# A hybrid attention block on one Trainium2 core: low-rank codes in 2 passes of 16, statistics ahead of the last depth step, ten leading matmuls of constants, a filled slot and one more pool

## The chip, the core and the metric

The kernel runs on one core of one Trainium2 chip. The core has TensorE (PE) for matrix products, VectorE (DVE) and ScalarE (ACT) for element work, GpSimd (POOL), which does next to nothing here, and SyncE (SP), on whose queue nearly all DMA transfers are issued. SBUF is the on-chip memory of 128 partitions that the engines work on, PSUM holds what PE writes, in banks of 128 x 512 float32. The metric is the time of one execution on the device in microseconds (us), the median of several runs. All runs shown are of one launch that computes one layer for 1024 tokens.

## What is computed

One encoder layer in float32 on x of 1024 tokens by 1024 features. The reference, cut to what matters here:

```python
h = _rms_norm(x, norm_mix_g[l])
proj = h @ w_in[l]
(g_q, g_k, g_v, g_r, g_lr_f, g_lr_b, s_q, s_k, s_v, gate_a, gate_b) = jnp.split(proj, split_at, axis=-1)
y_gla = _gla_branch(g_q, g_k, g_v, g_r, g_lr_f, g_lr_b, ...) @ w_o_gla[l]
y_swa = _swa_branch(s_q, s_k, s_v, ...) @ w_o_swa[l]
merged = jax.nn.sigmoid(gate_a) * y_gla + jax.nn.sigmoid(gate_b) * y_swa
x = x + merged @ w_out[l]
h2 = _rms_norm(x, norm_ffn_g[l])
gu = h2 @ w_ffn_in[l]
x = x + (jax.nn.silu(gu[..., :D_FF]) * gu[..., D_FF:]) @ w_ffn_out[l]
```

Inside the GLA branch the gate of each direction is `z = lr @ up + bias`, with `lr` the low-rank code of a token: 16 numbers for the forward and 16 for the backward direction, so 32 columns of `w_in`. Its log-sigmoid is summed along chunks of tokens and scales q and k of four heads. The SWA branch is windowed attention with 8 query heads.

## The kernel before

Matrix products are kept at float32 precision by splitting each operand into a high part of type float32r and a low part, the rest. A product is three matmuls (`mm3`, lines 74 to 77): high by high, low by high, high by low. All take 128 rows of depth, mostly 128 x 512 results; the kernel has 7880. Weights arrive as units of 128 x 512 through `wunit` (lines 62 to 69): SP loads `wr` (4 buffers), ACT copies the high part `wh` (5), DVE subtracts to get the low part `wl` (5). x lies transposed, as `xh[k][s]` and `xl[k][s]`: depth step k of 8 by token half s of 2.

The stages, in order:

- The **lead**. ACT and DVE split x depth step by depth step, with the gain of the norm, while PE multiplies it with the weights of q and k of head 0 into four banks `bq[m][s]` (m is 0 for q, 1 for k). x itself is squared on ACT (`x_square`) and summed on DVE into `acc`. The norm's factor is applied to results, so it is needed only then: `norm_stats` (lines 117 to 121) multiplies `acc` with a matrix of ones, one fp32 matmul for each half, and `rsqrt` makes `rstd`. Eight small matmuls (`vt`) give the same factor by token, `rstdt`. The low-rank codes (`lr_mm`, lines 247 to 253) stand around this: the 32 columns are repeated three times to 96, in two weight units of four depth steps; each step and half takes three matmuls, 48 in all, 24 ahead of the statistics and 24 behind. `lr_out` multiplies with `rstd` and writes `lrS`: rows 0 to 31 the high part, 32 to 63 the low part, 64 to 95 the high part again, and two rows of ones for the bias. The gates' matmul then reads all 98 rows of `lrS` against `upS`, which holds the up-projection as high, high and low. The first gates' matmul of the program is a mark in what follows.
- The **GLA slots**. The other projections are generators in the list `dense`, 2400 matmuls, which `fill(n)` draws from one by one. The GLA of 4 heads by 8 chunks is cut into small steps, and `slot(stages, n)` (line 230) runs the steps of one time slot with n dense matmuls spread between them: 40 in slots 0 to 5, 31 in slots 6 to 34, and 18 in slots 35 to 44. Ahead of slot 0 stand 24 dense matmuls. A slot without a step returns without any fill. There are two such: slot 1, and slot 43, between the last step back through the chunks (`g_back_out`, whose last ACT instruction scales `ob`, line 484) and the last turn (`g_turn`, line 490, whose transposes read `ob`).
- The **SWA slots**, with 60, 46 or 28 dense matmuls each, and what is left of `dense` behind them.
- The **projections of the branches and the output**. `prep_a` (lines 766 to 777) loads the GLA's output `o` and the gate `r` for each of eight depth steps into pairs of buffers (`lo`, `lr`), which lie in memory that the SWA stage frees, and writes the parts `oah` and `oal` that the next matmuls read.
- **FFN in**, by seven products of half blocks in place of eight (Strassen's way): x1 is combined into the operands 11, 21, T1, 22, T2, T3 and T4, each as high and low parts of four depth steps, 16 KB in a partition. They lie in three pools: `big1` (11, 21; 32 KB), `big2` (T1, 22, T2; 48 KB) and `big3` (T3, T4). For each of 22 feature tiles `ffn_in` runs T1, T2, 21, 11 of the next tile, T3, 22, T4.
- **FFN out**, likewise, in groups of 132 matmuls (line 1029). Once the big pools close, `fo1`, `fo2` and `fo3` take their memory from the same start. `fo1` holds six buffers `hr` for loads of activations (12 KB) and eleven weight tiles `a11` (22 KB), 34 KB; `fo2` and `fo3` hold the parts `hh` and `hl` (lines 1001 and 1002) and further weights.

The order of PE is the order of the code (`manual_schedule`). The orders of ACT, DVE and SP are made by the tile scheduler. Each engine works its own queue strictly in order and waits at semaphores for the others. A tile in memory that another pool had before waits for that pool's last reader there.

Of the kernel before, what the change touches and what calls it, by code (L numbers as in the profile page):

```python
# [8 lines left out]
F32 = mybir.dt.float32  # L9
# [5 lines left out]
P = 128  # L15
# [8 lines left out]
NB = 7  # L24
PAD = 672
# [4 lines left out]
def body(tc, i, out):  # L30
    nc = tc.nc
    with ExitStack() as root:
# [90 lines left out]
        def fgroup(units, xa, xb, nk):  # L123

            b = [mmtile(), mmtile()]
            k = 0
            for src, ku in units:
                h, l = wunit(src, ku * P)
                for kk in range(ku):
                    c = slice(kk * P, (kk + 1) * P)  # L130
                    st, sp = k == 0, k == nk - 1
                    mm(b[0], h[:, c], xa[k][0], st, False)
                    mm(b[0], h[:, c], xb[k][0], False, False)
                    mm(b[1], h[:, c], xa[k][1], st, False)
                    mm(b[1], h[:, c], xb[k][1], False, False)
                    mm(b[0], l[:, c], xa[k][0], False, sp)
                    mm(b[1], l[:, c], xa[k][1], False, sp)
                    k += 1
            return b

# [89 lines left out]
        def slot(stages, n):  # L230

            stages = [f for f in stages if f]
            done = 0
            for j, f in enumerate(stages):
                f()
                t = n * (j + 1) // len(stages)
                fill(t - done)
                done = t
# [8 lines left out]
        def lr_mm(b, u):  # L247
            h, l = wunit(i["w_lr"][u], 384)
            for kk in range(4):
                k = u * 4 + kk  # L250
                c = slice(kk * 96, (kk + 1) * 96)
                for s in range(2):
                    mm3(b[s][:96], h[:, c], l[:, c], xh[k][s], xl[k][s], k == 0, k == KT - 1)

        def lr_out(b):
            lrf = ip.tile([96, T], F32, tag="lrf", name="lrf")
            for s in range(2):
                c = slice(s * HT, (s + 1) * HT)
# [21 lines left out]

        with tc.manual_schedule(engines={mybir.EngineType.PE}):
            bq = [[mmtile(), mmtile()] for _ in range(2)]

# [3 lines left out]
            for k in range(KT):  # L287
# [924 lines left out]
```

## Time and profile before

| | us |
|---|---|
| median of 3 runs | 1688.89 (1688.65 to 1688.97) |
| span of the profiled execution | 1687.4 |
| PE busy, 7880 matmuls | 1670.9 |
| DVE busy, 2454 instructions | 1181.0 |
| ACT busy, 1939 instructions | 869.3 |

The profile shows one execution. It gives no time of its own for that execution beside the span; the runs lie 1.2 to 1.6 us above it. A matmul's end is modelled in the trace, so PE's busy time says less than the distance between the starts of its matmuls. In the rows of the timeline the first number is the start in us, the second the length, then engine, line, operation, what is written and read with the shape, and in brackets how long the engine was idle before and what released it. Names are those of the program without buffer numbers.

### The profile page before, as it was taken

How to read it: one execution, taken by the hardware profiler on the slowest of the kernel's cores; microseconds unless marked ns; L12 is line 12 of the kernel's file. 1: busy time of each engine (PE TensorE's matmuls, PEld its weight loads, DVE VectorE, ACT ScalarE, POOL GpSimd, SP SyncE). 2: the span in 40 equal slices, each digit the busy share in tenths (PEclk: the TensorE clock that was granted, in tenths of full speed). 3: DMA queues.
4: the chain of work that ended last, by engine and by line, in shares of the span. 5: the costliest groups of instructions: out<-in, count | busy, mean ns of one | idle time of the engine just before them, and what ended most of it. 6: DMA issues, size and time to landing. Idle time of an engine off the chain costs nothing.

```text
span 1687.4 us, 23673 instructions
## 1 busy us (share of the span) xinstructions
PE 1670.9 (99%) x7880; PEld 1390.1 (82%) x7880; DVE 1181.0 (70%) x2454; ACT 869.3 (52%) x1939; POOL 0.2 (0%) x4
## 2 busy tenths in 40 slices
PE   8999999999999999999999999999999999999999
PEld 6788888888788888888888888888888888788887
DVE  7767777764578666546674468987778877779755
ACT  7554767776557656544553466533333333354443
POOL 0000000000000000000000000000000000000000
PEclk9999999999999999999999999999999999999999
DMA  6533434444533233247764645344224443496433
GB/s 197 157 113 109 123 126 140 131 141 125 175 121 118 83 100 96 74 150 245 235 213 146 188 129 187 113 134 134 94 88 156 163 143 132 152 333 200 146 100 119
DMA packets 153738, 245.85 MB, mean 146 GB/s; under 512 B 17582, under 2 KB 43054, under 8 KB 153616
## 3 DMA queue, kind: packets, MB, share of 16 engines
q1 hardware_dynamic: 153616, 244.34, 45.6%
q8 instruction: 62, 1.02, 0.3%
q14 instruction: 60, 0.49, 0.1%
HBM read 177.17 MB, written 67.11 MB: 145 GB/s over the span
## 4 chain that ended last, share of the span: by engine, by line
PE 97%; DVE 2%; ACT 1%; DMA 0%; issue 0%; SPq 0%; ACTq 0%; DVEq 0%
PE mm L72 48%; PE ch L72 9%; PE mm L1029 7%; PE mm L884 6%; PE mm L882 6%; PE mm L883 6%; PE ch L1029 5%; PE ch L884 2%; PE ch L882 2%; PE ch L883 2%; PE ch L664 1%; PE ch L490 0%; PE ch L614 0%; PE ch L405 0%; DVE cs L364 0%
## 5 line engine op out<-in xcount | busy, mean ns | idle before, releaser
L66 ACT ACTIVATE wh<-wr 128x512 fp32r<-128x512 f32 (+1 forms) x256 | 160.1, 628 | 173.6 <-PE mm L72 149.5
L68 DVE TENSOR_TENSOR wl<-wr,wh 128x512 fp32r<-128x512 f32 (+1 forms) x256 | 174.9, 687 | 89.0 <-ACT wh L66 82.2
L72 PE MATMUL mm<-xh,wh 128*128 128x512 f32 x512 | 203.3, 397 | 5.9 <-ACT wh L66 5.9
L72 PE MATMUL mm<-xl,wh 128*128 128x512 f32 x512 | 203.4, 397 | 0.0
L72 PE MATMUL mm<-xh,wl 128*128 128x512 f32 x512 | 169.4, 397 | 0.0
L72 PE MATMUL mm<-wh,xh 128*128 128x512 f32 x320 | 126.7, 396 | 1.9 <-DVE st L146 1.2
L72 PE MATMUL mm<-wl,xh 128*128 128x512 f32 x320 | 127.3, 398 | 0.0
L72 PE MATMUL mm<-wh,xl 128*128 128x512 f32 x320 | 126.4, 395 | 0.0
L72 PEld LDWEIGHTS mm<-xh,wh 128*128 128x128 f32 x512 | 96.7, 189 | 22.4 <-ACT wh L66 5.9
L856 ACT ACTIVATE wh<-ws 128x512 fp32r<-128x512 f32 x88 | 55.7, 634 | 115.2 <-PE mm L883 69.3
L72 PEld LDWEIGHTS mm<-xl,wh 128*128 128x128 f32 x512 | 96.7, 189 | 16.9
L72 PEld LDWEIGHTS mm<-xh,wl 128*128 128x128 f32 x512 | 94.9, 189 | 16.7 <-DVE wl L68 0.2
L856 ACT ACTIVATE wh<-a 128x512 fp32r<-128x512 f32 x66 | 41.9, 635 | 90.9 <-PE ch L1029 42.2
L856 ACT ACTIVATE wh<-wr 128x512 fp32r<-128x512 f32 x52 | 33.0, 635 | 91.1 <-issue 49.5
L857 DVE TENSOR_TENSOR wl<-a,wh 128x512 fp32r<-128x512 f32 x66 | 45.5, 690 | 41.8 <-ACT wh L856 41.6
L72 PEld LDWEIGHTS mm<-wh,xh 128*128 128x128 f32 x320 | 60.2, 188 | 14.0 <-DVE st L146 1.6
L1029 PE MATMUL mm<-hh,wh 128*128 128x512 f32 x176 | 69.3, 394 | 1.6 <-ACT hh L1001 1.6
L1029 PE MATMUL mm<-hl,wh 128*128 128x512 f32 x176 | 69.1, 393 | 0.5 <-DVE hl L1002 0.5
L1029 PE MATMUL mm<-hh,wl 128*128 128x512 f32 x176 | 69.2, 393 | 0.1
L647 ACT ACTIVATE p<-p,nm,rs 128x384 f32<-128x384 f32 (+1 forms) x64 | 42.9, 673 | 50.3 <-DVE nm L641 50.3
L72 PEld LDWEIGHTS mm<-wh,xl 128*128 128x128 f32 x320 | 60.2, 188 | 10.4
L857 DVE TENSOR_TENSOR wl<-ws,wh 128x512 fp32r<-128x512 f32 x88 | 60.3, 685 | 11.9 <-ACT wh L856 11.9
(508 smaller groups left out, 4419.8 us busy)
## 6 DMA issues: line engine op xcount, KB each, us to landing
wr<-in_w_fi_dram SPq DMA_DIRECT2D x102, 256.0 KB, 2.9
wr<-in_w_t_dram SPq DMA_DIRECT2D x80, 256.0 KB, 2.8
wr<-in_w_f_dram SPq DMA_DIRECT2D x64, 256.0 KB, 2.7
B<-c SPq DMA_DIRECT2D x44, 256.0 KB, 2.1
T<-tx SPq DMA_DIRECT2D x44, 256.0 KB, 2.4
a<-in_w_fo_dram SPq DMA_DIRECT2D x44, 256.0 KB, 5.3
hr<-T SPq DMA_DIRECT2D x44, 256.0 KB, 2.7
hr<-B SPq DMA_DIRECT2D x33, 256.0 KB, 4.3
```

The lines of the kernel that those rows point to most:

```text
L66: nc.scalar.activation(h, raw, AF.Copy)
L68: nc.vector.tensor_tensor(l, raw, h.bitcast(F32), op=ALU.subtract)
L72: nc.tensor.matmul(o, a, b, start=start, stop=stop)
L647: nc.scalar.activation(p[:, h, :w], p[:, h, :w], AF.Exp, bias=nm_[:, h:h + 1], scale=a.rs[:, h:h + 1], accum_out=dn[:, h:h + 1])
L664: nc.tensor.transpose(pt[:, h], a.p[:, h, (kb - a.b0) * P:(kb - a.b0 + 1) * P], ident)
L856: nc.scalar.activation(h, src, AF.Copy)
L857: nc.vector.tensor_tensor(l, src, h.bitcast(F32), op=ALU.subtract)
L882: nc.tensor.matmul(o, h[:, c], x[kk][0], start=start and kk == 0, stop=False, skip_group_check=True)
L883: nc.tensor.matmul(o, h[:, c], x[kk][1], start=False, stop=False, skip_group_check=True)
L884: nc.tensor.matmul(o, l[:, c], x[kk][0], start=False, stop=kk == nk - 1, skip_group_check=True)
L1029: nc.tensor.matmul(ys[m], a[:, c], b, start=f0, stop=f1, skip_group_check=True)
```

## The change

There are five parts.

1. The 32 columns of the low-rank codes are loaded once as 128 x 8 x 32 and split into `lrhl`, high and low side by side. For each depth step and half one matmul takes 64 columns (high and low against `xh`) and one 32 columns (high against `xl`): 32 matmuls. `lr_out` then adds rows 32 to 63 to rows 0 to 31, by way of a copy on ACT, before it multiplies with `rstd`, and writes the two high copies and the low part of `lrS`.
2. `norm_stats` stands ahead of depth step 7 of q and k (a new function `qk_mm`), and all of the codes' matmuls come behind that step, in one piece, then `vt`.
3. Ten fp32 matmuls of 128 x 128, ones by ones, stand first on PE. They write a bank that q and k overwrite later.
4. A slot without a step draws its n dense matmuls.
5. T1 lies in a pool of its own, `big4`, between `big1` and `big2`.

The unused function `fgroup` is deleted.

```diff
--- before.py
+++ after.py
@@ -22,6 +22,7 @@
 NFF = 22
 NA = 4
 NB = 7
+WARM = 10
 PAD = 672
 
 QKM = ("q0", "k0", "q1", "k1", "q2", "k2", "q3", "k3")
@@ -119,24 +120,6 @@
                 v = chtile((P, HT))
                 mm(v, ones, acc[:, s * HT:(s + 1) * HT], True, True)
                 rsqrt(rstd[:, s * HT:(s + 1) * HT], v, 1.0 / T, EPS, epst, pool, (P, HT), "rs")
-
-        def fgroup(units, xa, xb, nk):
...
 
         def proj_f_out(name, b):
             for s in range(2):
@@ -231,6 +214,8 @@
 
             stages = [f for f in stages if f]
             done = 0
+            if not stages:
+                fill(n)
             for j, f in enumerate(stages):
                 f()
                 t = n * (j + 1) // len(stages)
@@ -244,21 +229,29 @@
         mask = gc.tile([P, 4, P], F32, tag="mask", name="mask")
         nc.vector.memset(mask, 1.0)
         nc.vector.memset(mask[:, :, 0:1], 0.0)
-        def lr_mm(b, u):
-            h, l = wunit(i["w_lr"][u], 384)
-            for kk in range(4):
-                k = u * 4 + kk
-                c = slice(kk * 96, (kk + 1) * 96)
+        def lr_mm(b):
+            raw = ip.tile([P, KT, 32], F32, tag="lrw", name="lrw")
+            nc.sync.dma_start(out=raw, in_=i["w_lr"])
+            hl = ip.tile([P, KT, 2, 32], FR, tag="lrhl", name="lrhl")
+            nc.scalar.activation(hl[:, :, 0], raw, AF.Copy)
+            nc.vector.tensor_tensor(hl[:, :, 1], raw, hl[:, :, 0].bitcast(F32), op=ALU.subtract)
+            for k in range(KT):
                 for s in range(2):
-                    mm3(b[s][:96], h[:, c], l[:, c], xh[k][s], xl[k][s], k == 0, k == KT - 1)
+                    st, sp = k == 0, k == KT - 1
+                    mm(b[s][0:64], hl[:, k].rearrange("p a b -> p (a b)"), xh[k][s], st, sp)
+                    nc.tensor.matmul(b[s][0:32], hl[:, k, 0], xl[k][s], start=False, stop=sp, skip_group_check=True)
 
         def lr_out(b):
-            lrf = ip.tile([96, T], F32, tag="lrf", name="lrf")
+            lrf = ip.tile([32, T], F32, tag="lrf", name="lrf")
+            lrt = ip.tile([32, T], F32, tag="lrt", name="lrt")
             for s in range(2):
                 c = slice(s * HT, (s + 1) * HT)
-                nc.vector.tensor_tensor(lrf[:, c], b[s][:96], rstd[:96, c], op=ALU.mult)
-            nc.scalar.activation(lrS[0:96], lrf, AF.Copy)
-            nc.vector.tensor_tensor(lrS[32:64], lrf[32:64], lrS[32:64].bitcast(F32), op=ALU.subtract)
+                nc.scalar.copy(lrt[:, c], b[s][32:64])
+                nc.vector.tensor_tensor(lrf[:, c], b[s][0:32], lrt[:, c], op=ALU.add)
+            nc.vector.tensor_tensor(lrf, lrf, rstd[0:32], op=ALU.mult)
+            nc.scalar.activation(lrS[0:32], lrf, AF.Copy)
+            nc.scalar.activation(lrS[64:96], lrf, AF.Copy)
+            nc.vector.tensor_tensor(lrS[32:64], lrf, lrS[0:32].bitcast(F32), op=ALU.subtract)
 
         xr = {}
 
@@ -278,8 +271,15 @@
             if k:
                 nc.vector.tensor_tensor(a, a, sq, op=ALU.add)
 
+        def qk_mm(k, s):
+            c = slice((k % 4) * P, (k % 4 + 1) * P)
+            for m in range(2):
+                mm3(bq[m][s], us[m][0][:, c], us[m][1][:, c], xh[k][s], xl[k][s], k == 0, k == KT - 1)
+
         with tc.manual_schedule(engines={mybir.EngineType.PE}):
             bq = [[mmtile(), mmtile()] for _ in range(2)]
+            for _ in range(WARM):
+                mm(bq[1][1][:, :P], ones, ones, True, True)
 
             x_load(0, 0)
             us = [wunit(i["w_f"][m, 0]) for m in range(2)]
@@ -290,11 +290,10 @@
                         x_load(k + 1, s)
                 if k == 4:
                     us = [wunit(i["w_f"][m, 1]) for m in range(2)]
-                c = slice((k % 4) * P, (k % 4 + 1) * P)
                 for s in range(2):
                     x_tile(k, s)
-                    for m in range(2):
-                        mm3(bq[m][s], us[m][0][:, c], us[m][1][:, c], xh[k][s], xl[k][s], k == 0, k == KT - 1)
+                    if k < KT - 1:
+                        qk_mm(k, s)
             for k in range(KT):
                 for s in range(2):
                     x_square(k, s)
@@ -302,13 +301,14 @@
             tri = load_const(gc, "tri", i["c_tri"], (P, P), U32)
             g2 = load_const(cst, "g2", i["g2"], (P, KT))
             og = load_const(cst, "og", i["og"], (P, 2))
+            norm_stats(acc, ip)
+            for s in range(2):
+                qk_mm(KT - 1, s)
             bl = [chtile((P, 512)), chtile((P, 512))]
-            lr_mm(bl, 0)
-            norm_stats(acc, ip)
+            lr_mm(bl)
             vt = chtile((P, KT, 2))
             for t in range(KT):
                 mm(vt[:, t], acc[:, t * P:(t + 1) * P], ones[:, 0:2], True, True)
-            lr_mm(bl, 1)
             proj_f_out("q0", bq[0])
             proj_f_out("k0", bq[1])
             rsqrt(rstdt, vt[:, :, 0], 1.0 / T, EPS, epst, ip, (P, KT), "rt")
@@ -725,7 +725,7 @@
                 YX["21"].append(bsplit(big1, f"b21{k}", b21))
             elif step == 1:
                 nc.vector.tensor_tensor(b12, b12, b11, op=ALU.subtract)
-                YX["T1"].append(bsplit(big2, f"bt1{k}", b12))
+                YX["T1"].append(bsplit(big4, f"bt1{k}", b12))
                 YX["22"].append(bsplit(big2, f"b22{k}", b22))
                 nc.vector.tensor_tensor(b22, b22, b12, op=ALU.subtract)
                 YX["T2"].append(bsplit(big2, f"bt2{k}", b22))
@@ -846,6 +846,7 @@
         bs.close()
         bigs = ExitStack()
         big1 = bigs.enter_context(tc.tile_pool(name="big1", bufs=1))
+        big4 = bigs.enter_context(tc.tile_pool(name="big4", bufs=1))
         big2 = bigs.enter_context(tc.tile_pool(name="big2", bufs=1))
 
 
@@ -1154,8 +1155,7 @@
     d["w_f"] = _units(np.concatenate(cols, axis=1), 4)
     wt = [w[:, 1024:1536], w[:, 1536:2048], w[:, 4128:4640], w[:, 3104:3616], w[:, 3616:4128]]
     d["w_t"] = np.ascontiguousarray(np.stack([a.reshape(KT, P, 512) for a in wt]))
-    lr = np.tile(w[:, 3072:3104], (1, 3)).reshape(2, 4, P, 96)
-    d["w_lr"] = np.ascontiguousarray(lr.transpose(0, 2, 1, 3)).reshape(2, P, 384)
+    d["w_lr"] = np.ascontiguousarray(w[:, 3072:3104].reshape(KT, P, 32).transpose(1, 0, 2))
     up = np.zeros((98, 2, 512), f)
     for g in range(3):
         up[g * 32:g * 32 + 16, 0] = n["gla_gate_up_fwd"][0]
```

How this moves instructions is seen at three places, with rows of the built programs' orders: line, operation, written<-read, shape. First PE in the lead, before: the end of the first 24 matmuls of the codes, the statistics, and the first of the second 24 (ch_377 and ch_376 are the codes' two banks, ch_408 and ch_418 those of the statistics).

```order
L72 MATMUL ch_377<-xh_97,wh_380 96x512
L72 MATMUL ch_377<-xl_113,wh_380 96x512
L72 MATMUL ch_377<-xh_97,wl_382 96x512
L72 MATMUL ch_408<-acc,ones 128x512
L72 MATMUL ch_418<-acc,ones 128x512
L72 MATMUL ch_428<-ones,acc 128x2 x8
L72 MATMUL ch_376<-xh_98,wh_439 96x512
```

And PE at the statistics now, in depth steps 6 and 7 of q and k (mm_136 to mm_139 are their banks; xh_103 and xl_119 are step 6, xh_104 and xl_120 step 7, of half 1 and half 0).

```order
L73 MATMUL mm_139<-xh_103,wh_258 128x512
L73 MATMUL mm_139<-xl_119,wh_258 128x512
L73 MATMUL mm_139<-xh_103,wl_260 128x512
L73 MATMUL ch_374<-acc,ones 128x512
L73 MATMUL ch_384<-acc,ones 128x512
L73 MATMUL mm_136<-xh_104,wh_252 128x512
L73 MATMUL mm_136<-xl_120,wh_252 128x512
```

Ahead of the statistics stand the q and k matmuls of step 6 now, no longer step 7 and 24 of the codes, and step 7 begins right behind them.

DVE at the last squares, before: the sums into acc, then the codes' low parts, then upS.

```order
L279 TENSOR_TENSOR acc<-acc,sq_353 128x512
L279 TENSOR_TENSOR acc<-acc,sq_356 128x512
L279 TENSOR_TENSOR acc<-acc,sq_359 128x512
L279 TENSOR_TENSOR acc<-acc,sq_362 128x512
L279 TENSOR_TENSOR acc<-acc,sq_365 128x512
L68 TENSOR_TENSOR wl_382<-wr_378,wh_380 128x384
L68 TENSOR_TENSOR wl_441<-wr_437,wh_439 128x384
L318 TENSOR_TENSOR upS<-upr,upS 34x1024
```

The same place of DVE now (sq_351 is the square of step 5, half 1; sq_360 and sq_363 those of step 7, half 0 and half 1; lrw and lrhl hold the columns of the codes).

```order
L272 TENSOR_TENSOR acc<-acc,sq_351 128x512
L237 TENSOR_TENSOR lrhl<-lrw,lrhl 128x8x32
L318 TENSOR_TENSOR upS<-upr,upS 34x1024
L272 TENSOR_TENSOR acc<-acc,sq_354 128x512
L272 TENSOR_TENSOR acc<-acc,sq_357 128x512
L272 TENSOR_TENSOR acc<-acc,sq_360 128x512
L69 TENSOR_TENSOR wl_525<-wr_521,wh_523 128x512
L272 TENSOR_TENSOR acc<-acc,sq_363 128x512
```

The subtractions for the codes and for upS stand ahead of the last four sums, and a weight's subtraction ahead of the very last.

DVE at the border of FFN in and FFN out, before: lines 958 to 969 make the last feature tile's outputs c from u and the products, line 1002 makes the low part of the activations of FFN out, line 857 that of its weights.

```order
L958 TENSOR_TENSOR c_3562_15609<-mm_15529,p_3551_15548 128x512
L961 TENSOR_TENSOR u_3555_15569<-ch_15528,u_3555_15569 128x512
L962 TENSOR_TENSOR u_3555_15569<-u_3555_15569,rstd 128x512
L964 TENSOR_TENSOR u_3555_15569<-u_3555_15569,rstd 128x512
L967 TENSOR_TENSOR c_3568_15649<-mm_15529,p_3529_15440 128x512
L969 TENSOR_TENSOR c_3562_15609<-c_3562_15609,u_3555_15569 128x512
L968 TENSOR_TENSOR c_3568_15649<-c_3568_15649,g_3558_15587 128x512
L1002 TENSOR_TENSOR hl_15687<-hr_15684,hh_15686 128x512
L857 TENSOR_TENSOR wl_15691<-a_3580_15682,wh_15690 128x512
```

DVE at the border now:

```order
L959 TENSOR_TENSOR c_3556_15604<-mm_15524,p_3545_15543 128x512
L858 TENSOR_TENSOR wl_15687<-a_3574_15678,wh_15686 128x512
L858 TENSOR_TENSOR wl_15711<-a_3580_15702,wh_15710 128x512
L962 TENSOR_TENSOR u_3549_15564<-ch_15523,u_3549_15564 128x512
L1003 TENSOR_TENSOR hl_15683<-hr_15680,hh_15682 128x512
L963 TENSOR_TENSOR u_3549_15564<-u_3549_15564,rstd 128x512
L1003 TENSOR_TENSOR hl_15707<-hr_15704,hh_15706 128x512
L1003 TENSOR_TENSOR hl_15734<-hr_15731,hh_15733 128x512
L965 TENSOR_TENSOR u_3549_15564<-u_3549_15564,rstd 128x512
L968 TENSOR_TENSOR c_3562_15644<-mm_15524,p_3523_15435 128x512
L970 TENSOR_TENSOR c_3556_15604<-c_3556_15604,u_3549_15564 128x512
L969 TENSOR_TENSOR c_3562_15644<-c_3562_15644,g_3552_15582 128x512
```

The weights' subtractions (line 858 now) come ahead of line 962, and the activations' (line 1003) right behind it, ahead of the last products of FFN in (968 to 970).

More of the change, by code (lines that the diff above doesn't have):

```diff
@@ L121, in norm_stats @@
                 rsqrt(rstd[:, s * HT:(s + 1) * HT], v, 1.0 / T, EPS, epst, pool, (P, HT), "rs")
-        def fgroup(units, xa, xb, nk):
[L125 to L139, printed above, removed]
         def proj_f_out(name, b):
```

## The prediction

> **What bounds the kernel now.** I read the chain of the page first, then PE's waits, then the clock by stretches, and last the rows around each place that the change touches.
>
> ```profile
> span 1687.4 us, 23673 instructions
> ...
> PE 97%; DVE 2%; ACT 1%; DMA 0%; issue 0%; SPq 0%; ACTq 0%; DVEq 0%
> ```
>
> The chain that ended last is PE for 97% of its length. DVE and ACT matter only where PE waits for them, and these are all of PE's waits (engine, line waited for, us in total, times, longest):
>
> ```profile
> PE mm L72 <- ACT wh L66: 5.9, 1, 5.9
> PE ch L490 <- ACT ob L484: 1.6, 1, 1.6
> PE mm L1029 <- ACT hh L1001: 1.6, 1, 1.6
> PE mm L72 <- DVE st L146: 1.2, 1, 1.2
> PE mm L72 <- DVE st L149: 0.7, 1, 0.7
> PE ch L72 <- DVE rt L96: 0.6, 1, 0.6
> PE mm L1029 <- DVE hl L1002: 0.5, 1, 0.5
> PE ch L72 <- DVE sl L420: 0.3, 1, 0.3
> ```
>
> They come to 12.4 us, of which 5.9 are the start. Beside waits PE loses time where its clock is halved. The windows view gives span and length of a stretch, then busy time with count of PE, PEld, DVE, ACT, POOL, the granted clock, DMA share and GB/s:
>
> ```profile
> 5.87:9.20 3.33, 3.33 (x8) 2.64 (x9) 2.65 (x4) 3.01 (x6) 0.00 (x0) 1.00 1.02 375
> 36.60:40.00 3.40, 2.75 (x21) 2.35 (x20) 1.67 (x4) 1.17 (x4) 0.00 (x0) 0.99 0.29 77
> 40.00:43.40 3.40, 3.40 (x9) 2.22 (x8) 3.30 (x8) 1.32 (x2) 0.00 (x0) 0.50 0.18 67
> 1469.50:1473.60 4.10, 1.92 (x6) 1.14 (x7) 3.47 (x7) 2.74 (x5) 0.00 (x0) 1.00 0.98 353
> 1473.60:1477.00 3.40, 3.40 (x10) 2.62 (x9) 3.40 (x7) 1.57 (x4) 0.00 (x0) 0.50 0.94 280
> ...
> 1504.07 29.92 PE ch L1029 x132
> ```
>
> The last row, from the chain in order of time, is the price of a matmul at full speed: 29.92/132 = 0.2267 us. From 5.87 to 9.20 only 8 ran, 0.42 each: PE starts at half speed. Two later windows of 3.4 us are at clock 0.50, and each follows a stretch in which PE stood or ran tiny matmuls. One such window costs half its length, 1.7 us. So what can be won is some 6.5 us of waits behind the start and 3.4 us of clock, beside matmuls that go away.
>
> **The lead.** The mark is the first matmul of the gates, which reads lrS and upS.
>
> ```profile
> 0.83 0.17 DVE L83 MEMSET ones<- 128x128 f32 x1 [0.83 <-PEq L1200]
> ...
> 26.65 0.39 PE L72 MATMUL mm<-xh,wh 128*128 128x512 f32 x1
> 29.37 0.39 PE L72 MATMUL ch<-xh,wh 128*96 128x512 f32 x1
> 34.91 1.88 PE L72 MATMUL ch<-acc,ones 128*128 128x512 f32 x4
> 37.43 1.95 PE L72 MATMUL ch<-ones,acc 128*128 128x2 f32 x16 [0.65 <-DVE rt L96]
> 53.39 0.40 PE L72 MATMUL ch<-lrS,upS 98*128 98x256 f32 x2
> ```
>
> Step 7 of q0 and k0 takes 29.37 - 26.65 = 2.72 us. The 24 low-rank matmuls of the first half take 34.91 - 29.37 = 5.54, 0.231 each with 96 columns, against 0.2267 with 128: width hardly counts. The 32 passes of 64 and 32 columns I price at 0.231, 7.4 us; if width counted in proportion they would cost 2.8, so the gain of leaving out 16 is 3.7, up to 8.3. I take 3.7, as 96 and 128 columns stand so close.
>
> Now the statistics come before step 7, and need all squares summed. On DVE and ACT (first and only row of each):
>
> ```profile
> 21.47 6.12 DVE L279 TENSOR_TENSOR acc<-acc,sq 128x512 f32<-128x512 f32 x10
> 28.55 1.22 DVE L318 TENSOR_TENSOR upS<-upr,upS 34x1024 fp32r<-34x1024 f32 x1
> 26.68 1.04 ACT L317 ACTIVATE upS<-upr 98x1024 fp32r<-98x1024 f32 x1
> 57.41 0.42 DVE L370 TENSOR_TENSOR e<-cs 128x256 f32<-128x256 f32 x1
> ```
>
> Ten additions run from 21.47, 0.61 each, and ended at 27.6 where nobody waited. In the new order of DVE the subtractions for the codes and for upS stand among them. Six additions end at 25.1; the codes' subtraction of 256 columns costs 0.42 by the last row; upS 1.22 makes 26.7; three more additions 28.6, the last of half 0. The last square of half 1 is late on ACT behind the upS copies (1.04 and another like it), so with a weight subtraction between, its sum is there at 29.8.
>
> PE ends step 6 at 26.65, or up to 1.5 us sooner if the ten leading matmuls take the start's half speed away. I take 1.0 sooner, 25.65, since x is split only about as fast as PE eats it. So **a new wait of some 3 us** stands before the statistics: half 0 28.6 to 29.5 (1.88 for both halves), half 1 to 30.7. What the leading matmuls win is swallowed by this wait: at the mark they are worth nothing. Are they hidden themselves? The nearest row is that of two 128x128 matmuls in 0.44 (at 439.80, below), so ten cost 2.2 us, 4.4 at half speed, from 1.0 (ones written) to 5.4, before 5.87. If each cost as much as one of 512 columns at half speed (1.88), they would end at 19.8, and push PE by 13.9 less the 3 of the wait; I take the nearer row.
>
> Then step 7 ends at 33.4, the codes at 40.8, the token statistics (1.9) at 42.7, the 24 dense matmuls ahead of the mark (5.4) at 48.1. The codes' way to lrS (two copies and additions, a product, two copies, a subtraction, 5.5 to 9 us with what DVE does between) has 7.3: I put the wait at 0.3, from 0 to 2. Mark at 48.4, without loss of clock. The waits for rt and st are gone from the sum: the statistics are done at 30.7, ten microseconds ahead of vt, and q0 and k0 leave their banks meanwhile.
>
> The clock stays. The window 36.60 to 40.00 had 2.75 of PE busy, in 16 tiny pieces besides, and the next was at 0.50. A wait of 3 us leaves PE busier by no more than that, so I expect a halved window behind it, 1.7 us: **mark at 50.1, gain 3.3.** [...]
>
> **The empty slots.** Slot 1 only takes its 40 dense matmuls earlier. Slot 43 stands at the end of the GLA:
>
> ```profile
> 437.76 0.40 PE L72 MATMUL mm<-xh,wh 128*128 128x512 f32 x1
> 439.80 0.44 PE L490 MATMUL ch<-ident,ob 128*128 128x128 f32 x2 [1.64 <-ACT ob L484]
> ```
>
> Between the last dense matmul and the turn PE lost 2.04 - 0.23 = 1.8 us. Now 18 dense matmuls, 4.1 us, stand there: **gain 1.8**, all of it, since the copy of ob needs no more than the 2.04. These 58 matmuls are missing later, in the end in the fill behind the last attention matmul, which falls from 190 to 144 by the new order of PE. That fill covers the preparation of the next stage:
>
> ```profile
> 743.92 0.39 PE L72 MATMUL ch<-ph,vSl 128*128 128x512 f32 x1
> 758.79 0.64 ACT L762 ACTIVATE oah<-lo 128x512 fp32r<-128x512 f32 x1 [0.23 <-DVE lo L776]
> 778.77 0.64 ACT L762 ACTIVATE oah<-lo 128x512 fp32r<-128x512 f32 x1 [1.31 <-DVE lo L776]
> 780.45 0.68 DVE L763 TENSOR_TENSOR oal<-lo,oah 128x512 fp32r<-128x512 f32 x1
> 787.49 0.39 PE L72 MATMUL mm<-oah,wh 128*128 128x512 f32 x1
> ```
>
> The rows are the last attention matmul, the high part of the second and the last of eight depth steps, the last low part, and the first matmul that reads them. The preparation starts when the attention's buffers come free, and ends 37.2 us after 743.92. PE came back after 43.57 (190 of 0.229) and needs the eighth step 21 matmuls, 4.8 us, later still. Now it comes back after 33.0, and needs the eighth at 37.8. That leaves 0.6 us, so I cost it at nothing; without that cover each microsecond that the preparation is longer would count in full.
>
> **The new pool.** At the border of the two FFN stages:
>
> ```profile
> 1460.94 0.39 PE L884 MATMUL mm<-b213h,wl 128*128 128x512 f32 x1
> 1466.38 0.39 PE L884 MATMUL ch<-b223h,wl 128*128 128x512 f32 x1
> 1466.80 0.33 SPq L1010 DMA_DIRECT2D a<-in_w_fo_dram  x1
> 1469.10 0.39 PE L884 MATMUL mm<-bt43h,wl 128*128 128x512 f32 x1
> 1469.83 0.63 ACT L856 ACTIVATE wh<-a 128x512 fp32r<-128x512 f32 x1 [0.93 <-DMA a<-in_w_fo_dram]
> 1471.08 0.50 PE L1029 MATMUL mm<-hh,wh 128*128 128x512 f32 x1 [1.59 <-ACT hh L1001]
> ```
>
> The load of the weight a goes out at 1466.80, as the last reader of 22 ends, because fo1 (34 KB) reached past big1 (32 KB) into the next pool. It lands 3.0 us later; ACT splits a, then hh, and PE starts 1.75 us late, waits again for hl, and gets a halved window. With T1 behind big1, the load waits for 21 (done at 1461.3) and T1, read earlier: 5.4 us sooner, a split by 1465. hh still lies over 22, so it is made from 1466.8 on, by 1467.8; hl, now ahead of the last products on DVE, by 1469.1. PE wants hh at 1469.33 and hl at 1469.56. Both are there: margin 0.5 us. From 1469.33 to 1504.07 are 34.74 us for the 132 matmuls that cost 29.92 in full flow: **gain 4.8**.
>
> **Sum.** 3.3 + 1.8 + 4.8 = 9.9 us off the profiled span of 1687.4: 1677.5. The median of the runs, 1688.89, is 1.5 above the span: **1679.0 us**.
>
> **Rivals.** (A) No halved window follows the new wait: three microseconds between full matmuls may be too little, unlike the 16 tiny ones. For it speaks that PE is busy to its brim before and after, against it the two windows above. 1.7 less: 1677.3. [...] (B) The tiny matmuls of vt halve a second window, as they did alone or with the 0.65 us wait before: 1680.7. (C) The border gives little: a or hl comes late, since on DVE two weight subtractions now stand ahead of u and hl, and one late load holds all behind it. With 3 to 4.8 of the gain lost: 1682 to 1683.8. (D) The change of order does its full work: the squares are in time, no new wait. Statistics at 25.65, mark at 45.3, gain 8.1: 1674.2. Against it stands the DVE sum, with 3 us between. (E) Slower: the preparation at the attention's end becomes the bound. Two depth steps go side by side, a pair in (778.77 - 758.79)/3 = 6.7 us; were they to go one by one, seven times 6.7 behind the first, which was done just before the second's 758.79, make some 62 us after the last attention matmul, and PE waits 24 us: 1703. It turns slower by more than 0.2% (3.4 us, what a measurement of this kernel tells from no change) from a preparation of 51 us on. Against it: nothing in the change touches its buffers, and fewer dense outputs stand beside it on ACT.
>
> **How the numbers follow.** Forecast 0.40 (own range 1677.5 to 1680.5, by the 0 to 2 of lrS and the 0.5 margins), A 0.20, B 0.14, C 0.12, D 0.06, E 0.04, others 0.04 (leading matmuls at the dear price, up to 1690, among them). The range takes in the first four, 1676.0 to 1683.8, which leaves 0.14 out. The lower end is A with narrow passes somewhat cheaper. Faster by over 0.2% is below 1685.5: all but E and the others, 0.92; same 0.04; slower 0.04.
>
> **What would show it.** The first real matmuls at 0.23 from about 5.9; a wait of PE for acc of 2 to 3 us before step 7, and none for rt or st; the mark near 50; 32 code matmuls in 7.4 us. Clock 0.50 in one window behind that wait (none is A, two are B). No wait for ob. At the border the load of a 5.4 us before 22's end, no wait for hh, clock full. Wrong would be: a wait for oah or oal at about 770 to 780, PE starting x after 6 us, or hl late at the border.

## The result, and the profile after

| | before | after |
|---|---|---|
| median of 5 runs, us | 1688.65 (1687.88 to 1688.97) | 1681.62 (1680.64 to 1682.41) |
| ratio, 95% interval | | 0.9956 (0.9944 to 0.9968) |
| span of the profiled execution, us | 1687.4 | 1678.9 |
| first gates' matmul, us | 53.39 | 50.23 |

The kernel became 7.0 us faster. The profiled execution after is the fastest of its five runs, so its span shows more, 8.5 us, than the medians do. Where the rest went is a matter of single executions, and the last experiments bear on it.

The waits of PE after, whole list (engine, line waited for, us in total, times, longest):

```profile
PE ch L73 <- DVE acc L272: 2.7, 1, 2.7
PE mm L73 <- DVE ones L84: 1.0, 1, 1.0
PE mm L1030 <- DVE c L968: 0.9, 1, 0.9
PE mm L73 <- ACT wh L67: 0.3, 1, 0.3
PE ch L73 <- DVE lrS L254: 0.3, 1, 0.3
PE ch L73 <- DVE pl L668: 0.2, 1, 0.2
PE mm L73 <- DVE xl L264: 0.2, 1, 0.2
```

All waits of before are gone but the start. Two of more than 0.3 us have come in their place: for acc ahead of the statistics, and for c, the last products of FFN in. In the lead, PE's timeline after (start, length, engine, line, operation, written<-read, shape):

```profile
1.04 4.52 PE L73 MATMUL mm<-ones 128*128 128x128 f32 x20 [1.04 <-DVE ones L84]
...
25.76 0.39 PE L73 MATMUL mm<-xh,wl 128*128 128x512 f32 x1
28.89 3.50 PE L73 MATMUL ch<-acc,ones 128*128 128x512 f32 x4 [2.74 <-DVE acc L272]
31.40 1.38 PE L73 MATMUL mm<-xh,wh 128*128 128x512 f32 x1
...
50.23 0.47 PE L73 MATMUL ch<-lrS,upS 98*128 98x256 f32 x2 [0.29 <-DVE lrS L254]
```

And DVE's, at the end of the sums:

```profile
25.24 0.41 DVE L237 TENSOR_TENSOR lrhl<-lrw,lrhl 128x256 fp32r<-128x256 f32 x1
25.68 1.22 DVE L318 TENSOR_TENSOR upS<-upr,upS 34x1024 fp32r<-34x1024 f32 x1
26.94 1.90 DVE L272 TENSOR_TENSOR acc<-acc,sq 128x512 f32<-128x512 f32 x3
28.75 0.68 DVE L69 TENSOR_TENSOR wl<-wr,wh 128x512 fp32r<-128x512 f32 x1
29.35 0.68 DVE L272 TENSOR_TENSOR acc<-acc,sq 128x512 f32<-128x512 f32 x1
```

PE has started its last matmul of step 6 at 25.76, which would let the next start at 26.0 (they start 0.23 apart), and stands until 28.89, when the last sum of half 0 is in; the subtractions for the codes and for upS lie between the sums. The clock follows (span, length, busy time and count of PE, PEld, DVE, ACT, POOL, granted clock, DMA share, GB/s):

```profile
25.80:29.20 3.40, 0.66 (x3) 0.30 (x2) 3.37 (x5) 3.35 (x6) 0.00 (x0) 1.00 0.00 0
29.20:32.60 3.40, 3.40 (x5) 1.28 (x4) 3.10 (x6) 2.09 (x4) 0.00 (x0) 0.50 0.52 118
```

At the border of the FFN stages, rows of SP, PE and DVE, and the next group of the chain:

```profile
1455.63 0.33 SPq L1011 DMA_DIRECT2D a<-in_w_fo_dram  x1
...
1463.37 0.39 PE L885 MATMUL mm<-bt43h,wl 128*128 128x512 f32 x1
1463.60 0.39 PE L1030 MATMUL mm<-hh,wh 128*128 128x512 f32 x1
1464.12 0.50 PE L1030 MATMUL mm<-hl,wh 128*128 128x512 f32 x1
...
1466.39 0.68 DVE L968 TENSOR_TENSOR c<-mm,p 128x512 f32<-128x512 f32 x1
1467.13 0.50 PE L1030 MATMUL mm<-hh,wh 128*128 128x512 f32 x1 [0.89 <-DVE c L968]
...
1495.31 29.92 PE ch L1030 x132
```

The load of a goes out 7.7 us ahead of the last matmul of FFN in (before: 2.3), and FFN out starts on the beat, 0.23 after the last matmul. It loses 0.3 to hl and 1.1 at the matmuls of the fourth bank: that bank held the last product of FFN in, which DVE reads only at 1466.39, behind hl. The other 0.4 is spread over the matmuls behind these two places, which start up to 0.34 apart. From 1463.60 to 1495.31 are 31.71 us for the work of 29.92, where before 34.74 went by.

### The profile page after: what moved, and what is told of

Same layout as the page of the kernel before. It is cut to its first block, busy times and chain, and to the rows that moved or that the text cites. A ratio compares the mean times of both kernels' runs of the same rounds, so it can differ in the third digit from the quotient of the medians.

```text
span 1678.9 us, 23670 instructions
## 1 busy us (share of the span) xinstructions
PE 1668.9 (99%) x7884; PEld 1387.8 (83%) x7884; DVE 1179.9 (70%) x2454; ACT 866.0 (52%) x1941; POOL 0.2 (0%) x4
## 4 chain that ended last, share of the span: by engine, by line
PE 96%; DVE 1%; ACT 1%; issue 1%; DMA 1%; SPq 0%; DVEq 0%; ACTq 0%
PE mm L73 48%; PE ch L73 9%; PE mm L1030 7%; PE mm L885 6%; PE mm L884 6%; PE mm L883 6%; PE ch L1030 5%; PE ch L885 2%; PE ch L884 2%; PE ch L883 2%; PE ch L664 1%; PE ch L490 0%; PE ch L614 0%; PE ch L405 0%; ACT xh L263 0%
## 5 line engine op out<-in xcount | busy, mean ns | idle before, releaser
L67 ACT ACTIVATE wh<-wr 128x512 fp32r<-128x512 f32 x254 | 158.6, 627 | 160.4 <-PE mm L73 146.5
L69 DVE TENSOR_TENSOR wl<-wr,wh 128x512 fp32r<-128x512 f32 x254 | 173.8, 686 | 87.7 <-ACT wh L67 82.4
L857 ACT ACTIVATE wh<-wr 128x512 fp32r<-128x512 f32 x52 | 32.9, 632 | 91.0 <-issue 49.3
L73 PEld LDWEIGHTS mm<-wh,xh 128*128 128x128 f32 x320 | 60.2, 188 | 11.1 <-ACT st L193 0.3
L73 PEld LDWEIGHTS mm<-wl,xh 128*128 128x128 f32 x320 | 60.2, 188 | 10.9
L73 PEld LDWEIGHTS mm<-wh,xl 128*128 128x128 f32 x320 | 60.2, 188 | 10.6
```

The costliest lines, as they stand in the source:

```text
L67: nc.scalar.activation(h, raw, AF.Copy)
L69: nc.vector.tensor_tensor(l, raw, h.bitcast(F32), op=ALU.subtract)
L73: nc.tensor.matmul(o, a, b, start=start, stop=stop)
L857: nc.scalar.activation(h, src, AF.Copy)
```

## The experiments

Each is the changed kernel with one edit, five runs, unless it says otherwise. "The mark" is the start of the first gates' matmul. The kernel before ran beside each: medians of 1688.79 to 1689.15. Two series of the unaltered changed kernel, the one above and `e12_again` below, have medians of 1681.62 and 1682.83. So a difference of some 1.2 us between two medians settles nothing by itself, and there the rows of the profiles have to decide; differences below are against 1681.62.

**The leading matmuls.** `e1_no_warm` and `e8_late_no_warm` leave them out, the second together with the statistics behind step 7 (below).

```diff
-WARM = 10
+WARM = 0
```

> The changed kernel without its ten leading matmuls. Theory (the wait for acc swallows what they win): the first matmuls of x run at half speed again, step 6 ends some 1 us later, near 26.8, the wait for acc shrinks from 2.7 to about 1.7 us, and the first gates' matmul stays at 50.2 (within 0.4); if the shorter wait leaves the clock alone it comes at 48.5. Time 1681.6, or 1679.9. Rival (they are worth their own microsecond): the mark at 51.2, time 1682.6.

> Statistics behind depth step 7 as in the run before (first gates' matmul at 46.3, 1679.0), and no leading matmuls. Theory (with no wait for acc to swallow it, the half speed of the start counts): the mark comes 0.8 to 1.1 us later, near 47.3, time 1680.0. Rival (they are worth nothing here either, since acc at 28.8 sets the statistics): the mark at 46.3 to 46.6, time 1679.0.

Measured: 1680.41 (1680.33 to 1682.75) and 1679.19 (1677.77 to 1682.26). PE in the lead of e1:

```profile
29.37 3.18 PE L73 MATMUL ch<-acc,ones 128*128 128x512 f32 x4 [2.08 <-DVE acc L272]
...
50.99 0.47 PE L73 MATMUL ch<-lrS,upS 98*128 98x256 f32 x2 [0.29 <-DVE lrS L254]
```

The wait for acc shrinks from 2.7 to 2.1 us, and the mark is 0.8 us later than in the first profile of the changed kernel and 0.3 later than in its second (50.71, below). In e8 it is at 46.76, 0.5 later than with the ten matmuls (46.30 in e2, below). Both marks lie between the two expectations. How much a mark varies by itself can be read from the runs whose lead is the same: 49.83 in e3, 50.24 in e4, 50.48 in e6, and with late statistics 46.28 in e10 and 45.95 in e11. The marks of e1 and e8 are later than all of these, by 0.3 to 1.2 and 0.5 to 0.8 us, so the ten matmuls are worth something like half a microsecond there. The times show no gain: 1.2 us less without the ten in e1, 0.2 more in e8, inside the spread of the runs.

**The place of the statistics.**

```diff
-            norm_stats(acc, ip)
             for s in range(2):
                 qk_mm(KT - 1, s)
+            norm_stats(acc, ip)
```

> The changed kernel with the statistics behind depth step 7 instead of ahead of it, and all else kept. Theory (the new wait stands only because PE asks for acc 2.7 us too early; step 7 is 2.7 us of work that covers it): the wait for acc falls under 0.6 us, no window at half clock follows, the first gates' matmul comes near 46 instead of 50.2, time about 1677.4. Rival (the early statistics are what took the waits for rt and st away): with them late these waits return, the mark is at 49 or later, time 1680.5 or more.

Measured: 1679.03 (1676.65 to 1679.40). PE in the lead of e2:

```profile
29.03 2.33 PE L73 MATMUL ch<-acc,ones 128*128 128x512 f32 x4
...
46.30 0.48 PE L73 MATMUL ch<-lrS,upS 98*128 98x256 f32 x2 [0.29 <-DVE lrS L254]
```

The statistics start at the same moment as in the changed kernel, 29.03 against 28.89, but with step 7 already done. No wait, no halved clock (1.0 over the execution), no wait for st, the mark 3.9 us sooner. The theory held; the rival (rt and st return) fell. The median shows 2.6 of the 3.9 us; this profile has a wait of 1.3 us for wl further on, which comes up again below.

**The codes.** `e5_old_codes` takes the 48 matmuls of 96 columns at the changed place, `e9_old_late` the same with the statistics behind step 7.

```diff
-            lr_mm(bl)
+            lr_mm(bl, 0)
+            lr_mm(bl, 1)
...
-                    mm(b[s][0:64], hl[:, k].rearrange("p a b -> p (a b)"), xh[k][s], st, sp)
-                    nc.tensor.matmul(b[s][0:32], hl[:, k, 0], xl[k][s], start=False, stop=sp, skip_group_check=True)
+                    mm3(b[s][:96], h[:, c], l[:, c], xh[k][s], xl[k][s], k == 0, k == KT - 1)
```

> The changed kernel with the 48 matmuls of 96 columns for the codes, in one piece at the changed place, and their old way to lrS. Theory (16 matmuls of 0.23 us are saved, but part is given back, since the scheduler set the codes' split and upS ahead of the last squares, which it does not do with the old codes): the wait for acc falls from 2.7 to some 1.6 us, the codes take 11.1 us instead of 7.4, the first gates' matmul comes 0.7 us (clock stays full) to 2.4 us (clock halves again) after 50.2, time 1682.3 to 1684.0. Rival (nothing is given back): the mark 3.7 us later, at 53.9, time 1685.3.

> The 48 matmuls of 96 columns for the codes and the statistics behind depth step 7, all else as changed. With e2 and e5 this closes a square: codes in 2 passes or 3, statistics early or late. Theory (the 16 passes left out are worth their 3 to 3.7 us only where the early statistics don't give them back): no wait for acc, the first gates' matmul at 48.4 to 49.8, which is 2 to 3.5 us behind the 46.3 of two passes with late statistics; time 1679 to 1681. Rival (two passes are worth nothing anywhere, since the chain to lrS ends as late): the mark at 46.3 to 47.

Measured: 1680.46 (1679.87 to 1682.02) and 1680.76 (1679.17 to 1681.42). PE in e5:

```profile
26.75 2.06 PE L73 MATMUL ch<-acc,ones 128*128 128x512 f32 x4 [1.19 <-DVE acc L264]
...
49.79 0.40 PE L73 MATMUL ch<-lrS,upS 98*128 98x256 f32 x2
```

The square of marks (e9's is the 48.48):

| mark, us | statistics ahead of step 7 | behind it |
|---|---|---|
| codes in 2 passes | 50.23 | 46.30 |
| codes in 3 passes | 49.79 | 48.48 |

I had expected that a part of the 3.7 us of passes is given back where the statistics come early. All of it was: with the old codes the last sums are not held up, the statistics start at 26.75, and 16 matmuls more end no later (the 0.4 us is inside what the mark varies by). Neither expectation of e5 held: the mark was forecast at 50.9 or later, and the time, 1.2 us below the changed kernel, at 1682.3 or more. The clock in e5's profile reads 0.95 all through and tells no window from another; that none was halved behind the wait is read from its matmuls, which start 0.23 apart from 28.9 on (0.43 in e1, where the clock reads 0.50). With the statistics late, two passes are worth 2.2 us at the mark, as expected. The median of e9 does not show the 1.3 us by which its mark is ahead of e5's; the spread found last is large enough to hide them.

**The order of DVE.** `e7_ups_after` moves the block of upS up in the text, behind the squares, and pins its ACT copy and its DVE subtraction behind what stands ahead of them.

```diff
+            tc.keep_in_program_order(nc.scalar.activation(upS, upr, AF.Copy))
+            tc.keep_in_program_order(nc.vector.tensor_tensor(upS[64:98], upr[64:98], upS[64:98].bitcast(F32), op=ALU.subtract))
...
             norm_stats(acc, ip)
```

> The changed kernel with the copies and the subtraction of upS pinned behind the last square on ACT and the last sum on DVE. Theory (of the wait for acc, 1.3 us is upS and the codes' split standing ahead of the last sums): acc is summed at 27.5, the wait is 1.5 us instead of 2.7, the first gates' matmul at 48.9, or 47.2 if the clock then stays full; time 1680.3 or 1678.6. Rival (upS moved back is late for the gates, or the rest of the chain to lrS is what ends last): the mark stays at 50.2.

Measured: 1680.20 (1679.60 to 1680.63). PE in the lead of e7:

```profile
28.27 1.98 PE L73 MATMUL ch<-acc,ones 128*128 128x512 f32 x4 [1.02 <-DVE acc L272]
...
47.91 0.48 PE L73 MATMUL ch<-lrS,upS 98*128 98x256 f32 x2 [0.29 <-DVE lrS L254]
```

The wait is down to 1.0 us, the clock stayed full (1.0 over the execution), and the mark is 2.3 us sooner. Of these, 0.6 is the earlier start of the statistics, and 1.7 the halved window that is gone (from there to the mark 19.6 us in place of 21.3). Step 6 ended 1.1 us later in this execution, at 26.9; counted from its end, the sums come 1.7 us sooner. The edit moves ACT's copies too, and the codes' subtraction went behind the sums along with upS; but DVE works without a pause from 21.63 in the changed kernel, and from 22.71 in e7, to the sum that PE waits for, so it is DVE's queue that sets its time. So the order of DVE makes most of the wait. Of the 2.3 us the median shows 1.4.

**The pool.** `e3_no_big4` puts T1 back.

```diff
-        big4 = bigs.enter_context(tc.tile_pool(name="big4", bufs=1))
...
-                YX["T1"].append(bsplit(big4, f"bt1{k}", b12))
+                YX["T1"].append(bsplit(big2, f"bt1{k}", b12))
```

> The changed kernel with T1 back in the pool of 22 and T2. Theory (the pool lets the first load of FFN out wait for 21 instead of 22): the wait of PE for hh of about 1.6 us and the window at half clock return at the border, the first 132 matmuls of FFN out take 34.7 us from the end of FFN in instead of 31.7, time 3 us more, 1684.6. Rival (the border is bound by hl and the last products whatever the pool): under 1 us more, below 1682.6.

Measured: 1685.06 (1683.10 to 1687.38, 11 runs), 3.4 us more. Two of the waits of PE in e3, and the second group of FFN out in its chain:

```profile
PE mm L1029 <- ACT hh L1001: 1.4, 1, 1.4
...
PE mm L1029 <- DVE hl L1002: 0.7, 1, 0.7
...
1500.03 29.92 PE ch L1029 x132
```

The waits for hh and hl are back, and, judging by the mean clock, a halved window behind them: the profiled run of e3 has 0.998, as that of before with its two, against 0.999 in the changed kernel with one. From the beat at which FFN in has ended, 1465.31, the first 132 matmuls take 34.72 us, against 31.71 with the pool. The pool is worth its 3 us.

**The banks at the border.** `e6_swap_banks` exchanges the two groups of banks in FFN out.

```diff
-            Z, X = banks(mmtile), banks(lambda: chtile((P, HT)))
+            Z, X = banks(lambda: chtile((P, HT))), banks(mmtile)
```

(and so for the later groups.)

> The changed kernel with the two groups of PSUM banks exchanged in FFN out, so that the first group of products writes banks that FFN in has left early. Theory (what is left of the border is PE's wait for the last product c, which still has to be read out of the fourth bank, behind hl on DVE): the wait for c of 0.9 us goes, the 132 matmuls end 1.1 us sooner after FFN in, time 1680.5. Rival (another wait, for hl, wh or a load, ends as late): unchanged, 1681.6.

Measured: 1680.50 (1679.09 to 1681.16). All waits of PE in e6:

```profile
PE ch L73 <- DVE acc L272: 2.7, 1, 2.7
PE mm L73 <- DVE ones L84: 1.0, 1, 1.0
PE ch L73 <- DVE lrS L254: 0.3, 1, 0.3
PE mm L73 <- DVE xl L264: 0.3, 1, 0.3
PE ch L73 <- DVE pl L668: 0.2, 1, 0.2
```

The wait for c is gone, and none took its place. The second group of FFN out in the chain of e6:

```profile
1493.77 29.92 PE mm L1030 x132
```

The first group starts at 1463.63, on the beat, and its 132 matmuls take 30.14 us, where 31.71 went by in the changed kernel and 34.74 before. With the banks exchanged the border gives 4.6 of the 4.8 us that were forecast. The median fell by the 1.1 us expected, though the runs of both overlap and the size is that of the difference between the two series of the changed kernel.

**The empty slots.** `e4_no_fill` draws nothing in them.

```diff
-            if not stages:
-                fill(n)
```

> The changed kernel with empty slots that draw nothing. Theory (18 dense matmuls cover the copy of ob): the wait of PE for ob of 1.6 us returns at the last turn of the GLA, time 1.8 us more, 1683.4. Rival (the 58 matmuls are missed at the end of the attention, so the fill only moves the loss): within 0.5 us of 1681.6.

Measured: 1682.94 (1681.91 to 1683.95), 1.3 us more, with these waits back (three of the nine in its list):

```profile
PE ch L488 <- ACT ob L482: 1.6, 1, 1.6
...
PE mm L73 <- DVE st L132: 0.7, 1, 0.7
...
PE ch L73 <- DVE sl L418: 0.3, 1, 0.3
```

They come to 2.6 us. The median is neither the 1.8 us up of the theory nor within 0.5 us as in the rival, and against the second series of the changed kernel it is only 0.1 us up. So the rows show that the drawn matmuls take these waits away; the times alone do not show what is left of the gain.

**What varies.** `e12_again` is the changed kernel unaltered.

> The changed kernel once more, unaltered, for what varies between executions. Theory (the spread of 1680.6 to 1682.4 comes from loads, in the wait for wl at some 840 us and the wait for c at the border, and not from the lead): the first gates' matmul at 50.2 within 0.5, the two later waits different from the 0 and 1.1 us of the first profile by half a microsecond or more. Rival (the lead varies, by one or two windows at half clock): the mark off by 1.7.

Measured: 1682.83 (1681.23 to 1685.34); the profiled execution took 1684.59. The mark is at 50.71, half a microsecond from the first profile's, so hardly any of the difference lies in the lead. One of its waits of PE:

```profile
PE mm L73 <- DVE wl L69: 2.0, 1, 2.0
```

The wait for c is 0.9 again, where a change of half a microsecond or more was expected. The one for wl, at 845 us in the projection of the second branch (the SWA's, first token half), was 0 in the first profile and is 2.0 here, and behind it the clock reads 0.51:

```profile
845.20:848.60 3.40, 1.37 (x6) 0.96 (x6) 3.15 (x6) 2.14 (x4) 0.00 (x0) 1.00 0.45 122
848.60:852.00 3.40, 3.40 (x10) 2.65 (x9) 3.40 (x7) 1.21 (x3) 0.00 (x0) 0.51 0.83 243
```

That is 3.7 us between two executions of one program, nearly all of the 3.9 by which their spans differ (1678.9 and 1682.8). DVE is busy without a gap there, with the preparation for the GLA's projection that comes next ahead of wl. The same wait was 0.2 in e1, 1.3 in e2, 1.5 in e3 and e5, 2.1 in e7, 1.0 in e8, 0.8 in e9, and 0 in e6. It was absent before and in e4, where nothing is drawn in slot 1.

The load behind it can be read from DVE's last pause ahead of wl, in the first profile of the changed kernel and in e12:

```profile
833.52 0.75 DVE L776 SCALAR_TENSOR_TENSOR lo<-lo,og,lr 128x512 f32<-128x512 f32 x1 [1.91 <-DMA lo<-o]
836.84 0.75 DVE L776 SCALAR_TENSOR_TENSOR lo<-lo,og,lr 128x512 f32<-128x512 f32 x1 [1.82 <-DMA lo<-o]
```

The pause is for the GLA's output of the second token half. It ends 8.3 us after the first matmul of the second branch's projection (825.27) in the one, 11.1 (after 825.76) in the other, and from there to wl DVE has hardly a gap. Over the 14 profiles PE's wait follows this lag: 0 up to 8.3 us, 0.2 at 9.3 (e1), 0.8 and 1.0 at 9.8 and 10.0 (e9, e8), 1.3 at 10.2 (e2), 1.5 at 10.6 (e3, e5), 2.0 and 2.1 at 11.1 and 11.2 (e12, e7). The three profiles with slot 1 empty, which leaves more matmuls to cover the preparation (before, e4, e11), have the three smallest lags, 6.3 to 7.4; the eleven others have 7.9 to 11.2. The load itself is not slower: from its start on SP's queue to the end of the pause it takes 4.3 us in the first profile and 4.2 in e12; it goes out later.

**Both mends, and slot 1.** `e10_late_swap` joins the edits of e2 and e6; `e11_late_swap_fill43` leaves slot 1 empty besides:

```diff
-            if not stages:
+            if not stages and n < 40:
                 fill(n)
```

> Statistics behind depth step 7 and the exchanged banks in FFN out together, the version that should beat both kernels. Theory (the two are in different stages and add): the first gates' matmul at 46.3, no wait for c at the border, time 1677.9, 3.7 us below the changed kernel. Rival (what is won ahead is lost where PE waits for wl at some 840 us, which took 0 to 2.1 us in the profiles so far): 1679 or more.

> As e10, with slot 43 filled alone and slot 1 left empty, so that 172 dense matmuls instead of 144 are left for the end of the attention. Theory (the wait for wl at some 840 us comes from the preparations behind the attention, which have 6.3 us more of cover now): no wait at 840 us, time 0.5 to 1.5 us below e10. Rival (that wait comes from loads and the order of DVE there, whatever the cover): the same as e10 within 0.5 us.

Measured: e10 1678.08 (1675.31 to 1679.50), e11 1675.52 (1674.92 to 1676.28). All waits of PE in e11:

```profile
PE mm L73 <- DVE ones L84: 1.0, 1, 1.0
PE mm L73 <- DVE st L132: 0.7, 1, 0.7
PE mm L73 <- ACT wh L67: 0.4, 1, 0.4
PE ch L73 <- DVE sl L420: 0.3, 1, 0.3
PE ch L73 <- DVE lrS L254: 0.3, 1, 0.3
```

Slot 1's 40 matmuls are the whole difference between the two. Drawn early, they save the waits for st and sl, 1.0 us together, which stood before and are back here. Left for the end of the attention, they leave no wait for wl in the profile of e11 (lag 7.4), and the runs spread by 1.4 us against 4.2 in e10. That the spread went with the wait is inferred, since e10's own profile, of a run of 1676.01, has no such wait either (lag 7.9). The median fell by 2.6 us where 0.5 to 1.5 was forecast, the two profiled spans differ by 0.5. e11 beats both kernels: 0.9922 of before (0.9908 to 0.9935), and its slowest run is 4.4 us below the fastest of the changed kernel in either series.

## Why the prediction was right, and where it was not

The sum was 9.9 us, from three terms. Against the profile they came to 3.2, 1.8 and 3.0, beside half a microsecond of small waits, and the medians of the two kernels lie 7.0 apart. So 1679.0 was 2.6 us too low, and 1681.62 lies above the forecast's own range of 1677.5 to 1680.5; the whole range holds it because it also takes in rival C.

*The lead, 3.3 us: right in size and in its steps.* The wait of some 3 us was 2.7, acc of half 0 came at 28.85 where 28.6 stood, half 1 at 30.0 where 29.8 stood, one window was halved (0.50 from 29.20 to 32.60), the codes took 7.4 us, and the mark stood at 50.23 against 50.1. That the leading matmuls are hidden (the last ended at 5.56, x began at 5.88) and worth nothing at the mark held within about a microsecond (e1). The first matmuls of x did not run at 0.23: ten start from 5.88 to 9.20, where eight did before, and step 6 ended 0.7 us sooner in place of 1.0, which the wait for acc swallowed. Only the statistics themselves took longer, 2.5 us to the next matmul where 1.9 was counted: the clock reads 0.50 from 29.20 on, 0.3 us behind their start. The order of DVE as the cause was argued; e7 and e5 show it.

*The halved clock, forecast against rival A.* It came in each profile with the wait of 2.7: the changed kernel's clock reads 0.50 behind it, in e4 and e6 the matmuls behind the statistics start 0.43 apart where 0.23 is full speed, and in e3 and e12 the statistics take 2.8 and 2.7 us to the next matmul, against 1.4 in e7. It came with 2.1 (e1, clock 0.50), and did not where the wait was 1.0 or 1.2 (e7 by its clock, 1.0 over the execution; e5 by the pace of its matmuls, 0.23).

*The empty slots, 1.8 us.* The wait for ob went, and returned in e4 with 1.6. What failed is the sentence on the cover: "That leaves 0.6 us, so I cost it at nothing". At that place it held: no wait for oah or oal. PE's and ACT's rows at the end of the attention after, as in the prediction:

```profile
748.62 0.39 PE L73 MATMUL ch<-ph,vSl 128*128 128x512 f32 x1
...
781.75 0.39 PE L73 MATMUL mm<-oah,wh 128*128 128x512 f32 x1
783.08 0.62 ACT L762 ACTIVATE oah<-lo 128x512 fp32r<-128x512 f32 x1
```

PE came back 33.1 us after the last attention matmul (33.0 was said), while ACT still had the last high part to do; before, that was done 8.1 us ahead (779.41 against 787.49). But the engines that prepare were now late for the next preparation, and wl stands behind that work in DVE's queue. The price, 0 to 2.1 us in the profiles and in e12 a halved window besides, falls 60 us further on. Rival E came nearest, but at the wrong place and much too dear: a preparation that runs late cost a few microseconds, not 24. Slot 1 also won what the prediction left out: the waits for st and sl.

*The border, 4.8 us: mis-sized, 3.0.* The load came 5.4 us sooner against the end of FFN in, as forecast (7.7 in place of 2.3 us ahead), and hh was on time. "Both are there: margin 0.5 us" failed for hl, 0.3 us late (in e12 hl came on the beat, and the wait for c was 0.9 all the same), and the term left out who else is queued behind hl: the read of the fourth bank. The prediction saw that hl had moved ahead of the last products on DVE, and took the gain without asking who waits for the products. That is rival C's kind of loss, with 1.8 of its 3 to 4.8 us. The clock stayed full, as forecast (1.00 from 1462.00 to 1468.00).

*The medians.* Runs of after stand 1.7 us above their own spans. By that offset the profile of before is of one of its slower executions, and that of after is of its fastest, so the sum, made from profile to median with 1.5, was some 0.2 short there. The rest of the 1.5 us between 8.5 and 7.0 fits the wait for wl, which the profile of after happens not to have; the other four runs were not profiled, so this is inferred from e12. The wait for wl is set by when one load goes out, as the lags above show. Why that load goes out 3 us later in some executions was not settled; in e12 and e7, the two longest, ACT stood 4.2 and 3.9 us for the load of a gate (ga) just ahead of it, and the others show no pause as long there.

## What to carry to other kernels

A gain is complete only when every reader behind the moved instruction has been asked as well: here hl passed the read of a bank, and upS passed the sums. Work that fills an early gap is taken from later cover, and its price can fall a stage beyond the place that it covered; here it came as a wait of 0 to 2.1 us that differs between executions, not as a fixed cost. Before a step is put ahead, see whether its operand is ready: the statistics started at the same moment early and late, and early they only left PE standing.

## What the runs showed of the hardware

The views of the traces show the granted clock at 0.50 in some stretches of 3.4 us, 40.00 to 43.40 and 1473.60 to 1477.00 before and 29.20 to 32.60 after, with 0.99 or 1.00 on both sides. PE had been little busy ahead of each. The stretches ahead of these and of two more, in e1 and e12, and what followed:

| run | stretch, us | PE busy in it, us (matmuls) | clock in the 3.4 us behind it |
|---|---|---|---|
| before | 36.60 to 40.00 | 2.75 (21, of them 16 of 128x2) | 0.50 |
| before | 1470.20 to 1473.60 | 1.92 (6) | 0.50 |
| after | 25.80 to 29.20 | 0.66 (3) | 0.50 |
| e1 | 27.30 to 30.70 | 1.25 (3) | 0.50 |
| e12 | 845.20 to 848.60 | 1.37 (6) | 0.51 |

The profile of e7 has a wait of 2.1 us in front of wl, where e12 has 2.0, and no halved clock behind it. Its idle time lies in the first two of these rows:

```profile
839.40:842.80 3.40, 3.06 (x14) 2.21 (x12) 3.40 (x7) 1.83 (x4) 0.00 (x0) 1.00 0.73 239
842.80:846.20 3.40, 1.60 (x7) 1.34 (x8) 3.40 (x6) 2.19 (x4) 0.00 (x0) 1.00 0.47 105
846.20:849.60 3.40, 3.40 (x17) 2.81 (x16) 3.40 (x7) 1.28 (x3) 0.00 (x0) 1.00 0.86 284
```

So neither the length of the wait nor PE's busy time tells alone what follows: of waits of 2.0 and 2.1 us one was followed by a halved clock and one was not, and 1.92 and 2.75 us of busy time were followed by one where 1.60 was not. None of the five stretches in the table was wholly idle. The ends of matmuls are modelled in the trace, so the busy times are rough, and what decides between the two cases these runs do not show.
